# One 512-wide pass over the high weights, and joined PSUM pools, in a two-layer decoder trunk

## The chip, the cores and the metric

The kernel runs on one core of a Trainium2 chip. The metric is device time in microseconds (us) of one execution, as the median of several. A profile of one execution shows every instruction of the core's engines: PE (TensorE, matrix products), PEld (its weight loads), DVE (VectorE), ACT (ScalarE), POOL (GpSimd) and SP (SyncE, which issues the DMAs).

## The reference

Two layers act on 256 tokens of width 1024, all in fp32. Each layer is a half-step gated feed-forward block (FFN), a parallel mixer of three branches, and a second FFN, each followed by a layer norm of the residual sum:

```python
for i in range(DEPTH):                                   # DEPTH = 2
    x = layer_norm(DN_ALPHA * x + 0.5 * swiglu(x, ffn1_gate[i], ffn1_up[i], ffn1_down[i]), ...)
    h = x @ w_in[i]                                      # 1024 -> 6144 columns
    z_gmlp, z_qk, z_v, z_s5, z_gate = jnp.split(h, SPLIT_IDX, axis=-1)
    y_a = gmlp_mixer(z_gmlp, ...)                        # causal spatial gating
    y_b = diff_attention(q, k, v, lam, ...)              # 4 heads, two softmaxes each
    y_c = s5_mixer(z_s5, ...)                            # state space, then y * sigmoid(y @ glu_w + glu_b)
    proj = jnp.einsum('blkw,kwd->blkd', jnp.stack([y_a, y_b, y_c], axis=2), w_branch[i])
    mix = jnp.sum(jax.nn.sigmoid(z_gate) * proj, axis=2) @ w_out[i]
    x = layer_norm(DN_ALPHA * x + mix, ...)
    x = layer_norm(DN_ALPHA * x + 0.5 * swiglu(x, ffn2_gate[i], ffn2_up[i], ffn2_down[i]), ...)
```

`swiglu` is `(silu(x @ wg) * (x @ wu)) @ wd` with an inner width of 2816.

## The kernel before

**Split products.** Every fp32 operand of a large product is split into a high part, rounded to the matrix engine's fp32r form, and a low part, the rest. A product of x and w is then three: low x by high w, high x by high w, high x by low w. The weights come from memory as 202 "pairs" of 1 MB (`fetch`, tile `raw`); ACT rounds each to `wh` (`round_hi`, two instructions of 128x1024), and DVE subtracts to get `wl` (`round_lo`, two of 128x1024). `wh` and `wl` have rings of four pairs, so these run some pairs ahead of PE.

**Three forms of product.** `xstat` and `kdown` keep the activations stationary and move 512 weight columns. `wstat`, the subject of the change, keeps a 128x128 block of weights stationary and moves the 256 tokens. For one block of 128 output features it runs over the K-tiles (8 of them for a depth of 1024, 4 for 512), with three products of 256 columns each. Its callers are `couple` (one pair, two blocks: FFN gates `pgc` and ups `puc`, and in the mixer `psu`, `ps5`, `psq` and the gates `psg`), `branch` (`psp`), `glu` (`psl`) and the third branch (`psc`). Two blocks share one PSUM tile of 128x512, and one ACT or DVE instruction takes both out, with the activation function where there is one.

**PSUM.** The eight banks are three pools: `acc` (4), `mm` (2, the products of `wstat`) and `tr` (2, transposes).

**Order.** There are no hand-written queues. Work is written as generators with priorities, and a `Scheduler` with its own cost estimates picks one operation after another and so fixes each engine's order when the program is built. Each engine then runs its list strictly in that order, and waits where an operand isn't there.

**The mixer.** After the columns of `psu`, `ps5` and `psq`, the main stream runs twelve gates `psg`, the branch products `psp`, the GLU product `psl` and the third branch `psc` in the order of the table `GATES`, then the output product (`ac` from `mix`). Beside it, attention (`pss`, `tra`, `po`, `tro`) and the state-space branch put work on DVE, ACT and PE. The state-space branch has four stages: `bu` on PE; on DVE four products `t` per half, two sums, the scans `gr` and `gi`, then `u`, `v` and the states `Hr`, `Hi`; then `py` on PE, eight ACT copies into `y`, and one DVE operation. After the second and the fourth stage `act_y` applies gelu to half of `y` on ACT and splits it; `glu` (`psl`) reads both halves.

Two lines say how the split products of one K-tile stood in `wstat`, and how a gate was taken out:

```python
b += [self.mmul(out, ws[k][0], x[1][:, k, :], k == 0, False),
      self.mmul(out, ws[k][0], x[0][:, k, :], False, False),
      self.mmul(out, ws[k][1], x[0][:, k, :], False, k == n - 1)]
...
yield A.activation(out=e, in_=ps, func=AF.Tanh, scale=0.5)
```

Of the kernel before, what the change touches and what calls it, by code (L numbers as in the profile page):

```python
# [75 lines left out]

def bundle(ops):
    return Op(ops[0].eng, [c for o in ops for c in o.calls], sum(o.cost for o in ops),
              [a for o in ops for a in o.ins], [a for o in ops for a in o.outs])
# [9 lines left out]
class Engine:  # L89
# [210 lines left out]
class Trunk:  # L300
    def __init__(self, ctx, tc, wst, x, lngb, lnt, glngb, s5p, s5bc, wsp, bsp, out):
# [7 lines left out]
        self.mm = pool("mm", bufs=2, space=PSUM)  # L309
        self.tr = pool("tr", bufs=2, space=PSUM)  # L310
# [6 lines left out]
        ya, yb, pl = ("YAh", "YAl"), ("YBh", "YBl"), [("L2", "L3"), ("P2", "P3")]  # L317
# [11 lines left out]
    def ps(self, pool, name, shape=(128, 512)):  # L329
        bufs = 4 if pool is self.acc else 2  # L330
        return Alloc(pool, pool.name, bufs, lambda: pool.tile(list(shape), F32, tag=pool.name, name=name))

    def free(self, *tiles):
        self.s.free(*tiles)


    def slab(self, i, tag, name, dt, bufs):

        if i in self.spare:
            tags = self.spare[i].pop(0)  # L340
            h = []
# [11 lines left out]
    def fetch(self):  # L353
        for i, w in enumerate(self.w):
            w.raw_tiles, w.raw = yield from self.slab(i if i in (2, 3) else -1, "raw", "raw", F32, 2)
            if len(w.raw_tiles) == 1 and i > 1:
# [68 lines left out]

    def couple(self, name):

        p = yield from self.pair()
        out = yield self.ps(self.mm, name, (128, 2, 256))
        for c in range(2):  # L430
            yield from self.wstat(out[:, c, :], self.blocks(p, c, 0, 8), self.xt)
        self.done(p)
        return out
# [91 lines left out]
    def ln_params(self, layer, i, box):  # L525
        for e, tg in enumerate(("P0", "P1")):
            g = yield self.t([128, 1024], tg, "ln" + "gb"[e])
            yield self.GQ.dma_start(out=g, in_=self.lngb[layer, i, e:e + 1, :].partition_broadcast(128))
            box["gb"].append(g)
        box["ev"].set()  # L530

    def norm(self, t, acc, xr, gb, final, evs=None):
# [38 lines left out]
        if t == 0:  # L571
            hi = yield self.t([128, 8, 256], "xh", "xh", F32R)
            lo = yield self.t([128, 8, 256], "xl", "xl", F32R)
            self.xt = (hi, lo)
        self.to_xt(x, t, gb["col"], gb["tr"][t])

    def affine(self, t, x, gb):
# [10 lines left out]
        if gb["left"] == 0:  # L588
            self.free(gain, bias)
# [38 lines left out]
    def ffn(self, layer, which, final):  # L628
# [49 lines left out]
        def gate(c, pg, box, ev):  # L678
            s = yield self.t([128, 2, 256], "t2k", "silc", bufs=3)
            yield A.activation(out=s, in_=pg, func=AF.Silu)  # L680
            self.free(pg)
            yield ev
            yield V.tensor_tensor(out=s, in0=s, in1=box[0], op=ALU.mult)
            self.free(box[0])
# [5 lines left out]
        for c in range(2, 11):  # L690
            pg = yield from self.couple("pgc")
            yield from new_h()
            box, ev = [], Event()
            self.s.spawn(gate(c, pg, box, ev), P_EVAC)
            pu = yield from self.couple("puc")
            box.append(pu)
            ev.set()
# [10 lines left out]
        self.free(*self.xt)  # L708
# [26 lines left out]
    def prep(self, layer, r):  # L735
# [69 lines left out]
        X, C = [], []  # L805
        for z, tg in zip("ri", ("P2", "P3")):
            x = yield self.t([128, 8, 128], tg, "X" + z)
            X.append(x)
        for z, tg in zip("ab", ("YAh", "YAl")):
            x = yield self.t([128, 8, 2, 64], tg, "C" + z)  # L810
            C.append(x)
# [3 lines left out]
        tm = yield self.t([128, 4, 16, 16], "YBh", "s5t4")  # L815
# [60 lines left out]
        self.free(tm, bc)  # L876

        WB = []
        for tg in ("YBh", "YBl"):
            x = yield self.t([128, 4, 2, 128], tg, "WB")  # L880
            WB.append(x)
# [20 lines left out]
        self.free(*WB, *X, *C)  # L902
# [51 lines left out]
    def gmlp(self, r, vn, uT, bsr, ya, evs, ev):  # L954
# [15 lines left out]
        self.free(vn, uT, bsr, r["wsT"])  # L970
        ev.set()

# [18 lines left out]
    def head(self, r, va, e, hs, st):  # L991
# [44 lines left out]
        if st["run"] == 0:  # L1036
            self.free(va)
# [96 lines left out]
    def s5_out(self, r, u5, U2, out):  # L1134
# [32 lines left out]
        self.free(u5, U2, r["k0"])  # L1167
# [10 lines left out]
    def mixer(self, layer, r):  # L1178
# [13 lines left out]
        ggb = []  # L1192
# [3 lines left out]
        def gparams():  # L1196
            for e, tg in enumerate(("P2", "P3")):
                g = yield self.t([128, 512], tg, "gg")
                yield self.GQ.dma_start(out=g, in_=self.glngb[layer, e:e + 1, :].partition_broadcast(128))
                ggb.append(g)  # L1200
# [8 lines left out]
        for t in range(2):  # L1209
            yield self.x_ev[t]  # L1210
            for b in range(2):
# [10 lines left out]
                else:  # L1222
                    if va is None:
                        va = yield self.t([128, 2, 512], "P1", "va")
                    s.spawn(self.evac(ps, va[:, t, :], None, va_ev[t]), P_EVAC)
        def free_gg():
            for e in evs:
                yield e
            self.free(vg, *ggb)
        s.spawn(free_gg(), P_PREP)  # L1230
        uT = yield self.t([128, 4, 256], "P0", "uT")
        evu = [Event(), Event()]
        for c in range(2):
            ps = yield from self.couple("psu")
            s.spawn(self.evac(ps, uT[:, 2 * c:2 * c + 2, :], AF.Gelu_apprx_tanh, evu[c]), P_EVAC)

        yh = yield self.t([128, 4, 256], "YAh", "yah", F32R)
        yl = yield self.t([128, 4, 256], "YAl", "yal", F32R)
        ya, ya_ev = (yh, yl), Event()

        s.spawn(self.gmlp(r, vn, uT, bsr, ya, evs + evu, ya_ev), P_EVAC)
        u5 = yield self.t([128, 4, 256], "P3", "u5")
# [365 lines left out]
```

## Time and profile before

| | us |
|---|---|
| median of 3 runs | 1230.9 (1230.32 to 1231.95) |
| the profiled execution | 1229.86 |
| its span, first to last instruction | 1228.1 |
| PE busy | 1214.4 (99% of the span) |
| DVE busy | 886.3 (72%) |
| ACT busy | 636.8 (52%) |

The profiled execution is 1.0 us below the median, and 1.8 us of it lie outside the span. "Busy" is the time in which at least one instruction of the engine was running; on DVE and ACT an instruction's record overlaps the next one's by a little, so a group's mean is longer than the step from one to the next. Of the span, the first FFN takes until about 201 us, the first mixer until 426, its second FFN until 617; the second layer repeats this.

### The profile page before, as it was taken

How to read it: one execution, taken by the hardware profiler on the slowest of the kernel's cores; microseconds unless marked ns; L12 is line 12 of the kernel's file. 1: busy time of each engine (PE TensorE's matmuls, PEld its weight loads, DVE VectorE, ACT ScalarE, POOL GpSimd, SP SyncE). 2: the span in 40 equal slices, each digit the busy share in tenths (PEclk: the TensorE clock that was granted, in tenths of full speed). 3: DMA queues.
4: the chain of work that ended last, by engine and by line, in shares of the span. 5: the costliest groups of instructions: out<-in, count | busy, mean ns of one | idle time of the engine just before them, and what ended most of it. 6: DMA issues, size and time to landing. Idle time of an engine off the chain costs nothing.

```text
span 1228.1 us, 21124 instructions
## 1 busy us (share of the span) xinstructions
PE 1214.4 (99%) x8734; PEld 1127.6 (92%) x8734; DVE 886.3 (72%) x1564; ACT 636.8 (52%) x980; POOL 16.2 (1%) x52
## 2 busy tenths in 40 slices
PE   8999999999999999999999999999999999999997
PEld 6999998999999889999889999989999998999996
DVE  6887658879996798775685544696899888744446
ACT  6445546567555664454464434376565447534340
POOL 1100000000000020000000000000000000000000
PEclk9999999999999999999999999999999999999999
DMA  8647655463456475766455555456445574655440
GB/s 311 240 174 262 219 205 226 176 247 137 168 202 239 181 258 180 254 227 211 174 204 204 201 175 204 171 200 238 181 146 207 188 240 170 235 180 199 177 171 35
DMA packets 42864, 246.18 MB, mean 200 GB/s; under 512 B 4880, under 2 KB 5648, under 8 KB 17424
## 3 DMA queue, kind: packets, MB, share of 16 engines
q1 hardware_dynamic: 42768, 244.84, 55.4%
q8 instruction: 68, 1.11, 0.4%
q14 instruction: 28, 0.23, 0.1%
HBM read 233.28 MB, written 11.53 MB: 199 GB/s over the span
## 4 chain that ended last, share of the span: by engine, by line
PE 97%; DVE 2%; DMA 0%; ACT 0%; issue 0%; DVEq 0%; SPq 0%
PE ac L203 23%; PE puc L203 17%; PE pgc L203 17%; PE psg L203 11%; PE psq L203 4%; PE psp L203 4%; PE pg L203 4%; PE pu L203 3%; PE psc L203 2%; PE psu L203 2%; PE ps L203 2%; PE pvg L203 2%; PE pva L203 2%; PE py L203 1%; PE psl L203 1%; PE trx L203 1%
## 5 line engine op out<-in xcount | busy, mean ns | idle before, releaser
L203 DVE TENSOR_TENSOR wl<-raw,wh 128x1024 fp32r<-128x1024 f32 (+2 forms) x416 | 481.4, 1190 | 192.6 <-ACT wh L203 185.1
L203 ACT CAST wh<-raw 128x1024 fp32r<-128x1024 f32 (+2 forms) x416 | 410.3, 1022 | 270.6 <-PE ac L203 88.2
L203 PE MATMUL pgc<-xl,wh 128*128 128x256 f32 x576 | 163.7, 284 | 0.0
L203 PE MATMUL puc<-xl,wh 128*128 128x256 f32 x576 | 163.3, 283 | 0.0
L203 PE MATMUL puc<-xh,wl 128*128 128x256 f32 x576 | 163.0, 283 | 0.0
L203 PE MATMUL puc<-xh,wh 128*128 128x256 f32 x576 | 163.0, 283 | 0.0
L203 PE MATMUL pgc<-xh,wh 128*128 128x256 f32 x576 | 163.0, 283 | 0.0
L203 PE MATMUL pgc<-xh,wl 128*128 128x256 f32 x576 | 163.0, 283 | 0.0
L203 PE MATMUL ac<-wh,hTl 128*128 128x512 f32 (+1 forms) x374 | 141.5, 378 | 0.0
L203 PE MATMUL ac<-wh,hTh 128*128 128x512 f32 (+1 forms) x374 | 141.3, 378 | 0.0
L203 PE MATMUL ac<-wl,hTh 128*128 128x512 f32 (+1 forms) x374 | 140.9, 377 | 0.0
L203 PE MATMUL psg<-xl,wh 128*128 128x256 f32 x384 | 111.8, 291 | 0.0
L203 PEld LDWEIGHTS pgc<-xh,wh 128*128 128x128 f32 x576 | 110.4, 192 | 1.0
L203 PEld LDWEIGHTS pgc<-xl,wh 128*128 128x128 f32 x576 | 110.4, 192 | 1.0
L203 PEld LDWEIGHTS puc<-xl,wh 128*128 128x128 f32 x576 | 110.6, 192 | 0.1
L203 PEld LDWEIGHTS puc<-xh,wh 128*128 128x128 f32 x576 | 110.6, 192 | 0.0
L203 PEld LDWEIGHTS puc<-xh,wl 128*128 128x128 f32 x576 | 110.6, 192 | 0.0
L203 PEld LDWEIGHTS pgc<-xh,wl 128*128 128x128 f32 x576 | 110.4, 192 | 0.0
L203 PE MATMUL psg<-xh,wh 128*128 128x256 f32 x384 | 108.6, 283 | 0.0
L203 PE MATMUL psg<-xh,wl 128*128 128x256 f32 x384 | 108.6, 283 | 0.0
L203 PEld LDWEIGHTS ac<-wl,hTh 128*128 128x128 f32 x374 | 70.3, 188 | 13.1
L203 PEld LDWEIGHTS ac<-wh,hTl 128*128 128x128 f32 x374 | 70.5, 188 | 12.3
(263 smaller groups left out, 2312.6 us busy)
## 6 DMA issues: line engine op xcount, KB each, us to landing
raw<-in_wst_dram SPq DMA_DIRECT2D x198, 1024.0 KB, 4.9
raw<-in_wst_dram SPq DMA_DIRECT2D x16, 256.0 KB, 5.4
tbd<-tabw SPq DMA_DIRECT2D x8, 512.0 KB, 6.8
tab<-tbd SPq DMA_DIRECT2D x8, 512.0 KB, 5.6
lng<-in_lngb_dram SPq DMA_DIRECT2D x6, 512.0 KB, 6.4
lnb<-in_lngb_dram SPq DMA_DIRECT2D x6, 512.0 KB, 7.2
wbd<-WB SPq DMA_DIRECT2D x4, 512.0 KB, 7.3
cf<-cd SPq DMA_DIRECT2D x8, 256.0 KB, 5.5
```

The source lines that it names most:

```text
L203: fn(**kw)
```

## The change

The two parts of x stand side by side in one tile (`Duo`: 128 x K-tiles x 2 x 256, low first), so one product of 512 columns does both parts against the high weights. It runs for all K-tiles first; then the 256-wide products with the low weights go on in the half of the PSUM tile that holds the high part. The block's result is the sum of the tile's two halves. `summed` makes it: ACT copies one half out of PSUM into a tile `cp` (128x256), and DVE adds the other half to it. The activation function then reads the sum from SBUF. So a block has a PSUM tile of its own, and each block brings one ACT copy and one DVE add, 280 of each in all.

The pools `mm` and `tr` become one of four tiles. Tiles of SBUF that held high and low parts apart are joined (`YA`, `YB`, `P01`, `P23`, `xx`), with the same work in them. The scheduler's estimate of a product's time is raised from 0.0025 + n/2400 to 0.0133 + n/2400, which moves instructions; the reserve for DMA descriptors is made smaller to give room.

```diff
+class Duo:
+    def __init__(self, tile):
+        self.tile = tile
+        self.parts = (tile[:, :, 1, :], tile[:, :, 0, :])
+    def both(self, k):
+        return self.tile[:, k, :, :]
...
-                return 0.0025 + n / 2400
+                return 0.0133 + n / 2400
...
-        self.mm = pool("mm", bufs=2, space=PSUM)
-        self.tr = pool("tr", bufs=2, space=PSUM)
+        self.mm = self.tr = pool("mm", bufs=4, space=PSUM)
...
-    def wstat(self, out, ws, x):
+    def wstat2(self, out, ws, x):
         n = len(ws)
-        for k0 in range(0, n, 2):
-            b = []
-            for k in (k0, k0 + 1):
-                b += [self.mmul(out, ws[k][0], x[1][:, k, :], k == 0, False),
-                      self.mmul(out, ws[k][0], x[0][:, k, :], False, False),
-                      self.mmul(out, ws[k][1], x[0][:, k, :], False, k == n - 1)]
-            yield bundle(b)
+        for k0 in range(0, n, 4):
+            yield bundle([self.PE.matmul(out=out, lhsT=ws[k][0], rhs=x.both(k), start=k == 0, stop=k == n - 1,
+                                         skip_group_check=True) for k in range(k0, k0 + 4)])
+        for k0 in range(0, n, 4):
+            yield bundle([self.PE.matmul(out=out[:, 0, :], lhsT=ws[k][1], rhs=x[0][:, k, :], start=False,
+                                         stop=k == n - 1, skip_group_check=True) for k in range(k0, k0 + 4)])
+
+    def couple2(self, name, box):
+        p = yield from self.pair()
+        for c in range(2):
+            out = yield self.ps(self.mm, name, (128, 2, 256))
+            yield from self.wstat2(out, self.blocks(p, c, 0, 8), self.xt)
+            box[c].append(out)
+            box[c][0].set()
+        self.done(p)
+
+    def summed(self, box, dst):
+        yield box[0]
+        ps = box[1]
+        cp = yield self.t([128, 256], "cp", "cp", bufs=2)
+        yield self.A.copy(out=cp, in_=ps[:, 0, :])
+        yield self.V.tensor_tensor(out=dst, in0=ps[:, 1, :], in1=cp, op=ALU.add)
+        self.free(ps, cp)
...
-            yield A.activation(out=s, in_=pg, func=AF.Silu)
+            for e in range(2):
+                yield from self.summed(pg[e], s[:, e, :])
+            yield A.activation(out=s, in_=s, func=AF.Silu)
...
+    def evac2(self, box, dst, func, ev, scale=1.0):
+        for e in range(2):
+            yield from self.summed(box[e], dst[:, e, :])
+        if func is not None:
+            yield self.A.activation(out=dst, in_=dst, func=func, scale=scale)
+        ev.set()
...
         def gate(b, m):
-            ps = yield from self.couple("psg" + str(b))
-            s.spawn(tanh(ps, e, ev), P_EVAC)
+            yield from self.couple_to("psg" + str(b), e, AF.Tanh, ev, 0.5)
```

The new order differs in many places; the ones below lie near the end of the first mixer, and the second has the same order there.

Before, on PE, around the last `py` of the state-space branch (the number behind a name is the buffer's):

```order
L203 MATMUL psg1_4145<-xh_2098,wl_3970 128x256
L203 MATMUL py_4179<-Hr_116,cf_4137 64x129 x2
L203 MATMUL py_4179<-Hi_117,cf_4137 64x129 x2
L203 MATMUL py_4179<-Hr_116,cf_4137 64x129 x2
L203 MATMUL py_4179<-U2_2491,k0_1095 32x128 x4
L203 MATMUL py_4179<-Hi_117,cf_4137 64x129 x2
L203 MATMUL psg1_4145<-xl_2099,wh_3938 128x256
L203 MATMUL psg1_4145<-xh_2098,wh_3938 128x256
```

66 products of the gates `psg` follow that `py` before the first `psl`. Now, on PE, at the same place:

```order
L217 MATMUL psg2_3854<-xx_1928,wh_3601 128x512 x8
L217 MATMUL psg2_3854<-xx_1928,wl_3651 128x256 x8
L217 MATMUL py_3915<-Hr_113,cf_3907 64x129 x2
L217 MATMUL py_3915<-Hi_114,cf_3907 64x129 x2
L217 MATMUL py_3915<-Hr_113,cf_3907 64x129 x2
L217 MATMUL py_3915<-uu_2302,k0_1041 32x128 x4
L217 MATMUL py_3915<-Hi_114,cf_3907 64x129 x2
L217 MATMUL psl_3945<-y5d_3198,wh_3680 128x512 x4
L217 MATMUL psl_3945<-y5d_3198,wl_3697 128x256 x4
```

All gates now stand ahead of the last `py`, and `psl`, which reads `y5d` (the split y), comes directly behind it.

Before, on DVE, from the last stage's scan `gi` to `Hi`:

```order
L203 SCALAR_TENSOR_TENSOR gi_3997<-pk_401,t3_3841 128x128 x4
L203 TENSOR_TENSOR u_4059<-gr_3996,tab_3836 128x512
L203 TENSOR_TENSOR v_4060<-gi_3997,tab_3836 128x512
L203 TENSOR_TENSOR wl_4031<-raw_3940,wh_4006 128x1024 x2
L203 TENSOR_TENSOR Hr_116<-u_4059,v_4060 128x4x128
L203 TENSOR_TENSOR u_4102<-gr_3996,tab_3836 128x512
L203 SCALAR_TENSOR_TENSOR part_4110<-th_3755,psp_4076 128x512
L203 TENSOR_TENSOR v_4103<-gi_3997,tab_3836 128x512
L203 SCALAR_TENSOR_TENSOR y5_2945<-u5_2490,spm_211,y5_2945 128x256
L203 TENSOR_TENSOR wl_4122<-raw_4022,wh_4077 128x1024 x2
L203 SCALAR_TENSOR_TENSOR part_4144<-th_4004,psp_4111 128x512
L203 TENSOR_TENSOR Hi_117<-u_4102,v_4103 128x4x128
```

Now, on DVE, the same stage:

```order
L217 TENSOR_TENSOR th_3827<-psg2_3854,cp_3887 128x256
L217 SCALAR_TENSOR_TENSOR gi_3873<-pk_385,t3_3755 128x128 x4
L217 TENSOR_TENSOR u_3899<-gr_3872,tab_3723 128x512
L217 TENSOR_TENSOR v_3900<-gi_3873,tab_3723 128x512
L217 SCALAR_TENSOR_TENSOR y5_2698<-uu_2302,spm_206,y5_2698 128x256
L217 TENSOR_TENSOR Hr_113<-u_3899,v_3900 128x4x128
L217 TENSOR_TENSOR u_3909<-gr_3872,tab_3723 128x512
L217 TENSOR_TENSOR v_3910<-gi_3873,tab_3723 128x512
L217 TENSOR_TENSOR Hi_114<-u_3909,v_3910 128x4x128
L217 TENSOR_TENSOR wl_3904<-raw_3842,wh_3886 128x1024 x2
L217 SCALAR_TENSOR_TENSOR y5_2698<-uu_2302,spm_206,y5_2698 128x256
L217 TENSOR_TENSOR y5d_3198<-y5_2698,y5d_3198 128x2x256
```

The add of `psg2_3854`, the product that stands right ahead of `py` on PE, now stands ahead of `gi`.

Now, on DVE, while PE runs the eight blocks of `psc` and comes to the output product, which reads the first two quarters of `mix` as `mix_4058`:

```order
L217 TENSOR_TENSOR pr_4129<-psc_4127,cp_4143 128x256
L217 TENSOR_TENSOR wl_4152<-raw_4069,wh_4128 128x1024
L217 TENSOR_TENSOR mix_4058<-part_3271,mix_4058 128x2x256
L217 TENSOR_TENSOR pr_4108<-psc_4114,cp_4158 128x256
L217 TENSOR_TENSOR wl_4152<-raw_4069,wh_4128 128x1024
L217 SCALAR_TENSOR_TENSOR th_3207<-th_3207,pr_4108 128x512
L217 TENSOR_TENSOR pr_4129<-psc_4142,cp_4161 128x256
L217 SCALAR_TENSOR_TENSOR part_3303<-th_3207,part_3303 128x512
L217 SCALAR_TENSOR_TENSOR th_3599<-th_3599,pr_4129 128x512
L217 TENSOR_TENSOR wl_4216<-raw_4136,wh_4189 128x1024 x2
L217 TENSOR_TENSOR mix_4058<-part_3303,mix_4058 128x2x256
```

Before, both quarters of that half of `mix` were split ahead of the third and the fourth weight pair of the output product; now both pairs (`wl_4152`, `wl_4216`) stand ahead of the second quarter.

## Rows read from the trace of the kernel before

**Rows 1.** The page's busy time, share of the span and instruction count by engine.
```profile
PE 1214.4 (99%) x8734; PEld 1127.6 (92%) x8734; DVE 886.3 (72%) x1564; ACT 636.8 (52%) x980; POOL 16.2 (1%) x52
```
**Rows 2.** The page's chain that ended last, shares of the span by engine.
```profile
PE 97%; DVE 2%; DMA 0%; ACT 0%; issue 0%; DVEq 0%; SPq 0%
```
**Rows 3.** The chain of waits in order of time: start us, us, what.
```profile
21.09 8.17 PE pu L203 x36
...
50.23 5.75 PE pgc L203 x48
...
61.74 5.47 PE ac L203 x24
```
**Rows 4.** Busy time by stretch: length, PE, PEld, DVE, ACT, POOL, clock, DMA share.
```profile
34.70:104.20 69.50, 69.50 (x550) 65.49 (x550) 57.19 (x145) 32.49 (x44) 0.00 (x0) 1.00 0.63 224
709.00:783.00 74.00, 74.00 (x553) 71.12 (x553) 35.87 (x35) 30.59 (x36) 0.00 (x0) 1.00 0.52 186
223.70:402.80 179.10, 179.02 (x1549) 173.46 (x1549) 147.03 (x305) 102.26 (x197) 0.00 (x0) 1.00 0.55 200
277.30:371.80 94.50, 94.42 (x825) 90.10 (x823) 88.08 (x218) 53.92 (x116) 0.00 (x0) 1.00 0.47 172
```
**Rows 5.** DVE and ACT groups by shape: count | busy us, mean ns of one.
```profile
L203 DVE TENSOR_TENSOR hTl<-trh,hTh 128x256 fp32r<-128x256 f32 x16 | 6.7, 422 | 7.9 <-ACT hTh L203 7.8
...
L203 ACT COPY at<-tra 128x256 f32<-128x256 f32 x8 | 2.9, 368 | 4.6 <-PE tra L203 4.6
```
**Rows 6.** DVE timeline, back-to-back runs of three shapes: start us, us, what.
```profile
279.25 1.74 DVE L203 TENSOR_TENSOR t<-bu,tab 128x256 f32<-128x256 f32 x5
...
288.42 1.29 DVE L203 TENSOR_TENSOR t<-t,t 128x512 f32<-128x512 f32 x2
...
290.08 2.36 DVE L203 TENSOR_TENSOR wl<-raw,wh 128x1024 fp32r<-128x1024 f32 x2
```
**Rows 7.** DVE timeline, third state-space stage, from the scan gi to Hi.
```profile
335.81 1.36 DVE L203 TENSOR_TENSOR_SCAN gi<-pk,t 128x128 f32<-128x128 f32 x4
...
340.59 0.69 DVE L203 TENSOR_TENSOR Hi<-u,v 128x512 f32<-128x512 f32 x1
```
**Rows 8.** The chain of waits from the last py to psl.
```profile
370.07 1.74 PE py L203 x24
371.81 8.11 PE psg L203 x66
379.92 5.65 PE psl L203 x48
```
**Rows 9.** ACT timeline after the last py.
```profile
371.85 2.21 ACT L203 COPY y<-py 32x128 f32<-32x128 f32 x8 [2.89 <-PE py L203]
...
374.69 0.62 ACT L203 ACTIVATE y<-y 128x512 f32<-128x512 f32 x1
...
376.15 0.62 ACT L203 CAST y5h<-y 128x512 fp32r<-128x512 f32 x1
```
**Rows 10.** DVE timeline after the last py.
```profile
374.10 0.49 DVE L203 SCALAR_TENSOR_TENSOR y<-u,spm,y 128x256 f32<-128x256 f32 x1 [3.04 <-ACT y L203]
...
377.42 0.69 DVE L203 TENSOR_TENSOR y5l<-y,y5h 128x512 fp32r<-128x512 f32 x1
```
**Rows 11.** Busy time by stretch at the end of the program.
```profile
1218.00:1222.00 4.00, 1.05 (x9) 0.84 (x8) 2.60 (x10) 0.00 (x0) 0.00 (x0) 1.00 0.00 0
1222.00:1228.00 6.00, 0.00 (x0) 0.00 (x0) 3.06 (x7) 0.00 (x0) 0.00 (x0) 0.57 0.25 87
```
**Rows 12.** PE timeline, the program's first 512-wide products.
```profile
7.60 0.57 PE L203 MATMUL pg<-wh,xl 128*128 128x512 f32 x1
8.01 0.40 PE L203 MATMUL pg<-wh,xh 128*128 128x512 f32 x1
...
9.66 0.40 PE L203 MATMUL pg<-wh,xh 128*128 128x512 f32 x1
9.89 0.40 PE L203 MATMUL pg<-wl,xh 128*128 128x512 f32 x1
```

More of the change, by code (lines that the diff above doesn't have):

```diff
@@ L329, in ps, with duo @@
     def ps(self, pool, name, shape=(128, 512)):
-        bufs = 4 if pool is self.acc else 2
-        return Alloc(pool, pool.name, bufs, lambda: pool.tile(list(shape), F32, tag=pool.name, name=name))
+        return Alloc(pool, pool.name, 4, lambda: pool.tile(list(shape), F32, tag=pool.name, name=name))
+    def duo(self, tag, name, n):
+        x = yield self.t([128, n, 2, 256], tag, name, F32R)
+        return Duo(x)
     def free(self, *tiles):
-        self.s.free(*tiles)
+        self.s.free(*(t.tile if isinstance(t, Duo) else t for t in tiles))
     def slab(self, i, tag, name, dt, bufs):
@@ L525, in ln_params @@
     def ln_params(self, layer, i, box):
[L526 to L529, printed above, removed]
+        g = yield self.t([128, 2, 1024], "P01", "lngb")
+        for e in range(2):
+            yield self.GQ.dma_start(out=g[:, e, :], in_=self.lngb[layer, i, e:e + 1, :].partition_broadcast(128))
+            box["gb"].append(g[:, e, :])
+        box["tile"] = g
         box["ev"].set()
@@ L690, in ffn @@
         for c in range(2, 11):
-            pg = yield from self.couple("pgc")
             yield from new_h()
[L693 to L697, printed above, removed]
+            pg, pu = ([[Event()] for _ in range(2)] for _ in range(2))
+            self.s.spawn(gate(c, pg, pu), P_EVAC)
+            yield from self.couple2("pgc", pg)
+            yield from self.couple2("puc", pu)
             if acc is None:
@@ L1196, in gparams @@
         def gparams():
[L1197 to L1200, printed above, removed]
+            g = yield self.t([128, 2, 512], "P23", "gg")
+            for e in range(2):
+                yield self.GQ.dma_start(out=g[:, e, :], in_=self.glngb[layer, e:e + 1, :].partition_broadcast(128))
+                ggb.append(g[:, e, :])
+            ggt.append(g)
             self.g_ev.set()
@@ L1287, in act_y @@
         def act_y():
-            for nm, tg in (("y5h", "P0"), ("y5l", "P1")):
-                z = yield self.t([128, 4, 256], tg, nm, F32R)
-                zz.append(z)
+            z = yield from self.duo("P01", "y5d", 4)
+            zz.append(z)
             for c in range(2):
@@ L1318, in branch @@
                 m = 2 * m2 + e
-                ps = yield self.ps(self.mm, "psp", (128, 2, 256))
-                for c in range(2):
-                    yield from self.wstat(ps[:, c, :], self.blocks(w, e, 4 * c, 4), (ya, yb)[b])
+                box = [[Event()] for _ in range(2)]
                 if b == 0:
@@ L1344, in glu @@
             w = yield from self.pair()
-            for nm, tg in (("ych", "P2"), ("ycl", "P3")):
-                x = yield self.t([128, 4, 256], tg, nm, F32R)
-                yc.append(x)
+            x = yield from self.duo("P23", "yc", 4)
+            yc.append(x)
             for e in z_ev:
@@ L1389, in mixer @@
         mx = []
-        for tg in (("YAh", "YBh"), ("YAl", "YBl")):
-            x0 = yield self.t([128, 4, 256], tg[0], "mixh", F32R)
-            x1 = yield self.t([128, 4, 256], tg[1], "mixl", F32R)
-            mx.append((x0, x1))
+        for tg in ("YA", "YB"):
+            x = yield from self.duo(tg, "mix", 4)
+            mx.append(x)
         h = []
@@ L1415, in mixer @@
             for mm in range(2):
-                ps = yield self.ps(self.mm, "psc", (128, 2, 256))
-                for c in range(2):
-                    yield from self.wstat(ps[:, c, :], self.blocks(w, mm, 4 * c, 4), yc)
-                s.spawn(third(2 * m2 + mm, ps), P_EVAC)
+                box = [[Event()] for _ in range(2)]
+                s.spawn(third(2 * m2 + mm, box), P_EVAC)
+                yield from self.blocks_to("psc", [self.blocks(w, mm, 4 * c, 4) for c in range(2)], yc[0], box)
             self.done(w)
```

165 lines of the change are left out of this document (84 added, 81 removed).

## The prediction

> **What bounds the kernel now.** I read the busy times first. PE is busy 99% of the span and DVE 72% [rows 1]. A busy PE need not be a PE at its pace, so the second view is the chain that ended last: 97% of it is PE's own work [rows 2]. The third is that chain in order of time, for the step from one product to the next. A run of 48 products of 256 columns takes 5.75 us, 0.1198 each; 24 of 512 columns take 5.47 us, 0.2279 each, and 36 of another 512-wide run 8.17 us, 0.2269 each [rows 3]. Twice the columns do not cost twice the time: two 256-wide products take 0.2396, one 512-wide 0.227 to 0.228. So some 0.012 us of each product are fixed, and fewer, wider products would shorten a kernel that PE bounds.
>
> The last view is busy time by stretch, to see who comes next. In the FFN of the second layer DVE is busy 35.9 of 74.0 us, and 57.2 of 69.5 where the preparation of the state-space tables lies beside the first FFN. In the mixer from `psu` to the output product it is busy 147.0 of 179.1, and from the first scores to the last `py` 88.1 of 94.5 [rows 4]. There DVE is nearly as full as PE, and it is not full of waits.
>
> **What PE saves.** The K-tiles of the stationary-weight products number 2016: 1152 in the FFNs (4 FFNs, 9 chunks, gate and up, 2 blocks of 8) and 432 in each mixer (12 gates, 4 q/k, 2 u and 2 state-space couples of 16, that is 320; `psp` 64, `psc` 32, `psl` 16). Each now costs 3 x 0.1198 = 0.3594, and will cost 0.2269 + 0.1198 = 0.3467 or, by the slower 512-wide run, 0.3477. That saves 0.0117 to 0.0127 us a K-tile, 23.6 to 25.6 us in all. I take 25, as the slow run holds a turn between two matrices that `wstat2` hasn't; 10.7 of it falls in the mixers.
>
> A rule of the Trainium skill speaks against this sum. "TensorE: Matmul & The Clock Gate", section "Wait — 56ns, not 53.3ns?", puts the fixed part of a matmul at about 2.5 ns. By it the change would save 2016 x 2.5 ns = 5 us instead of 25. The two runs above show about 12 ns, so I go by the rows.
>
> **What the evacuation adds.** 280 blocks bring one ACT copy and one DVE add of 128x256 each. The nearest rows are an ACT copy out of PSUM of that shape, 0.368, and a DVE operation of that shape with one operand in PSUM, 0.422 [rows 5]. Back to back, five DVE operations of this shape take 1.74, a step of 0.33 [rows 6]. So DVE gets 280 x 0.33 = 92 us more, ACT some 280 x 0.37 = 104 at most. Silu, tanh and the multiplications stay, with the same sizes. In the FFNs the adds are covered: a chunk has 4, 1.3 us, in the 17 us in which PE does three pairs, and even beside the preparation 57.2 + 16 x 0.33 = 62.5 stay under 69.5 less some 3. `gate`'s result is used two chunks later, and the last chunk's after three pairs of the down product, 8 us, against about 4 us of chain. I cost the FFNs at nothing; if the cover failed, PE would wait at the weights' low parts there. The joined PSUM pool, the joined tiles and the DMA reserve move no work by themselves: nothing.
>
> In each mixer there are 68 blocks, 22.4 us more of DVE: 147.0 + 22.4 = 169.4, in a stretch that PE would now do in 179.1 - 5.3 = 173.8. DVE would have to run at 97% through a chain of waits on other engines. Where this reaches PE is seen in the order. Three places, per layer:
>
> *The last state-space stage.* The add of the gate product `psg2_3854` stands ahead of `gi` on DVE, so `gi` can't start before PE has finished that product; `Hi` needs `gi`; `py` needs `Hi`; `psl` needs the split y; and on PE nothing stands between `psg2_3854`, `py` and `psl`. So this whole chain is a wait of PE. By rows: copy 0.37, add 0.42; from `gi` to the end of `Hi` the third stage has the very same sequence, 335.81 to 340.59 + 0.69, that is 5.47 [rows 7]; the part of `py` (1.74) after its first 4 of 24 records, 1.45 [rows 8]; eight copies 2.21, gelu 0.62 and cast 0.62 on ACT [rows 9]; the y operation 0.49 and the split 0.69 on DVE [rows 10]. Sum 12.34, with eight hand-offs of some 0.06 (371.81 to 371.85, 374.59 to 374.69 [rows 8 to 10]) 12.8. Two `psl` products need only the first half of y, so PE would in the meantime have done `py` and these, 1.74 + 0.46. **Wait: 10.6 us.** Before, the 66 products behind `py` (8.11 us [rows 8]) hid the end of this chain, and `Hi` did not wait for a product just ahead of `py`. The bounds: 9.5 if records overlap more, 12.5 if DVE comes late to the add.
>
> *From `psc` to the output product.* The first `psc` block ends 1.4 us after T, its start, and with the copies DVE begins on its adds at about T + 2.4. Until the second quarter of `mix` is split its list holds 7 adds (0.33), 9 operations of 128x512 (step 0.60) and 6 halves of weight pairs (step 1.17, as half of 2.36) [rows 6]: 2.3 + 5.4 + 7.0 = 14.7, so T + 17.1. PE has eight blocks of 1.39 and one pair of the output product, 24 products in 5.47 for both halves of the tokens, so 2.73 [rows 3]: T + 13.9. It waits 3.2. The fourth quarter comes 2 adds, 5 operations, a cast of 0.62 and a pair later, 6.6, when PE has done two pairs, 5.5: 1.1 more. **Wait: 4.3**, between 2 (ACT ahead, adds earlier) and 6.
>
> *From the first scores to that last stage.* 36 adds, 11.9 us, come in here, PE does 240 K-tiles 2.9 us faster, and DVE has 94.5 - 88.1 = 6.4 us of idle time to give [rows 4]: 8.4 us short. The weight pairs are made some two pairs ahead, which takes up most of it, but attention's transposes are not. **Wait: 2**, between 0 and 8.
>
> *The clock.* PE will stand idle twice for over 4 us around the last `py`. At the end of the program the granted clock is 1.00 up to 1222 us, and 0.57 in the mean after it, when PE had had nothing for three microseconds [rows 11], that is the lower of the two levels for most of it. At the program's start the first 512-wide products follow 0.41 us apart and later ones 0.23 [rows 12]. So the products after these waits may run at 1.2 GHz instead of 2.4 for a while. No row shows for how long after such a wait: between nothing and all 32 K-tiles of `psl` and `psp` at twice the time, 11 us. I take **2**, nearer to the start, where the slow step is gone within 2 us of these products.
> The Trainium skill, "TensorE: Matmul & The Clock Gate", section "What's actually happening", says that an idle PE is throttled to half its clock, and sustained work lifts this; the end of this trace agrees. Without it this term is 0 and the sum 4 us lower.
>
> **The sum.** 1229.86 (the profiled execution) - 25 + 2 x (10.6 + 4.3 + 2 + 2) = 1242.7. The median of the runs lies 1.0 above the profiled one: 1243.7, I say **1244**, 1.1% slower. The change breaks even at waits of 12.5 us a layer. Less than 0.2%, 2.5 us, can't be told from no change.
>
> **The rivals.**
> *Only the last state-space stage costs.* Against 4.3 + 2 + 2 stands that a wait of 10 us lets ACT and the weight pairs run ahead, and what is late behind it may then be hidden. For it: the `mix` wait rests on my counting of steps, and no row shows the two others. Then 1230.9 - 25 + 21.2 = 1227, faster; below 12.5 us a layer it decides the sign. Chance 0.13, including 0.02 for no wait at all (1206), which the order excludes as far as I can see.
> *About even.* One of the smaller terms falls in full: 1228.4 to 1233.4. Chance 0.09.
> *The wide product isn't cheaper.* If the 512-wide product of two parts takes as long as two of 256 columns (0.2396), nothing is saved, the change doesn't do what it says, and the waits remain: 1230.9 + 38 = 1269. The runs in [rows 3] speak against it, though none has stationary weights and 512 columns of x. Chance 0.04. The Trainium skill's 2.5 ns ("TensorE: Matmul & The Clock Gate", section "Wait — 56ns, not 53.3ns?") lies on this side, and would give 1264.
> *DVE bounds the mixers throughout.* If the 32 us of idle time that DVE has in the mixer now [rows 4] all stay, since they are waits on others, the mixer takes 179.1 + 22.4 = 201.5, and PE waits 27.7 a layer: 1230.9 - 25 + 55 = 1261. Chance 0.08.
> The forecast, 1234 to 1257, has 0.66. So slower 0.78, same 0.09, faster 0.13. Low bound: the one-stall case, 1227. High bound: the waits at their upper ends short of the last rival, 1258.
>
> **What would show it.** Right: `pgc` as 8 products of 0.227 and 8 of 0.120 in 2.78 us, FFN chunks of 16.6 us instead of 17.0; on PE, in each mixer, a wait for DVE at `py` of about 5 us and one at `psl` of about 5; waits at `ac` for `mix`; a granted clock under 1 behind them; DVE busy near 980. Wrong: `py` without a wait on `Hi`; a step of 0.24 in the wide pass; PE waiting in the FFNs for `wl`. The forecast is most open in the three small terms, of which I have only bounds.

## The result: 1265.8 us, 2.8% slower

The changed kernel takes 1265.8 us (4 runs, 1263.2 to 1267.2) against 1230.9; the ratio is 1.0283, 95% interval 1.0271 to 1.0295. The forecast was slower, 1244, with a range up to 1258: the sign held and the size did not. The profiled execution took 1267.2, its span 1265.5.

The page's busy times, against [rows 1], and the shares by engine of the chain that ended last, against [rows 2]:

```profile
PE 1214.4 (96%) x6718; PEld 1032.4 (82%) x6718; DVE 983.2 (78%) x1844; ACT 726.8 (57%) x1248; POOL 13.8 (1%) x52
...
PE 64%; DVE 21%; ACT 6%; DMA 6%; issue 2%; SPq 0%; DVEq 0%; ACTq 0%
```

PE has 2016 products fewer and is busy exactly as long: most of what the wide pass saved came back as slower products (8.9 us in each mixer, worked out below). Only 64% of the chain is PE's now, and DVE holds 21% of it. DVE is busy 97 us longer (983.2 - 886.3; 92 were forecast).

Where the 37 us lie is seen by stages. The table gives the time on PE's timeline from the first product of a stage to that of the next: the first FFN (counted from the start of the span), the first mixer (with its output product), the two FFNs between the mixers, the second mixer, and the last FFN up to its last down products.

| us | first FFN | mixer 1 | two FFNs | mixer 2 | last FFN |
|---|---|---|---|---|---|
| before | 200.8 | 224.9 | 379.8 | 224.9 | 166.4 |
| after | 201.6 | 247.9 | 373.4 | 248.1 | 163.1 |

The mixers lose 23 us each, the later FFNs gain 9.7, the first one nothing.

What PE waits for in the first mixer (view of waits: us in total, times, longest). Before, it had no such wait; the last two lines are all that PE waited for in that whole execution:

```profile
PE py L217 <- DVE Hi L217: 10.9, 3, 8.1
...
PE psl L217 <- DVE y5d L217: 3.7, 1, 3.7
...
PE ac L217 <- DVE mix L217: 2.7, 1, 2.7
...
PE trx L203 <- DMA x<-in_x_dram: 4.1, 2, 3.6
PE pg L203 <- DVE xl L203: 0.3, 1, 0.3
```

The chain of waits in order of time (start us, us, what), over the long wait of the first mixer and, last, over a chunk of the third FFN:

```profile
381.98 2.25 DVE wl L217 x2
384.23 0.34 DVE th L217
384.57 1.28 DVE gi L217 x4
...
389.27 0.70 DVE Hi L217
...
390.05 3.21 PE py L217 x24
393.28 0.27 ACT y L217
...
397.34 0.70 DVE y5d L217
398.04 0.04 issue
398.09 4.24 PE psl L217 x14
...
678.36 5.56 PE pgc L217 x32
683.92 5.59 PE puc L217 x32
689.51 5.47 PE ac L217 x24
```

The chunk takes 16.62 us, as forecast (16.6); by [rows 3] two runs of 48 and one of 24 came to 16.97.

Above it is the predicted chain, link for link: the last gate's add (`th`), the scan `gi`, `Hi`, `py`, eight copies, the split y, `psl`. One link was not in it: the halves of a weight pair, 2.25 us, stand ahead of the add. And `py` takes 3.21 us, not 1.74. The stretches around the waits say why; the seventh number of a row is the granted clock:

```profile
275.00:280.00 5.00, 5.00 (x31) 3.84 (x30) 2.80 (x4) 2.16 (x8) 0.00 (x0) 0.54 0.89 329
280.00:284.00 4.00, 4.00 (x22) 2.93 (x22) 2.04 (x11) 2.35 (x4) 0.00 (x0) 0.72 0.71 268
...
382.00:390.00 8.00, 0.00 (x0) 0.00 (x0) 7.97 (x15) 2.98 (x4) 0.00 (x0) 0.66 0.56 194
390.00:393.20 3.20, 3.15 (x25) 2.06 (x25) 2.23 (x2) 0.00 (x0) 0.00 (x0) 0.50 0.02 5
393.20:398.10 4.90, 1.20 (x5) 0.48 (x3) 1.18 (x2) 3.36 (x10) 0.00 (x0) 0.50 0.96 353
398.10:402.00 3.90, 3.90 (x13) 3.32 (x14) 0.42 (x1) 0.88 (x2) 0.00 (x0) 0.54 0.23 95
402.00:406.00 4.00, 4.00 (x25) 3.47 (x24) 2.31 (x5) 2.77 (x7) 0.00 (x0) 1.00 0.01 2
...
428.00:432.00 4.00, 4.00 (x13) 3.13 (x12) 3.96 (x7) 2.52 (x3) 0.00 (x0) 0.62 0.64 246
```

Behind each of three waits (1.9 us at the first `py`, 8.1 at the last, 2.7 at the output product) PE works for a while at a granted clock down to 0.50, the lower of the two levels (1.2 GHz of 2.4). Busy time times (1 - clock), over the six stretches in which PE works at it, gives 2.3 + 1.1 + 1.6 + 0.6 + 1.8 + 1.5 = 8.9 us a layer. (The 0.6 lies ahead of the wait at `psl`, which ends with DVE's split y: at the full clock it would have been spent waiting.)

(A slip in the part on the change: the products with the low weights go on in the half of the PSUM tile that holds low x, `out[:, 0, :]`. No time hangs on it.)

### The profile page after: what moved, and what is told of

Same layout as the page of the kernel before. It is cut to its first block, busy times and chain, and to the rows that moved or that the text cites. A ratio compares the mean times of both kernels' runs of the same rounds, so it can differ in the third digit from the quotient of the medians.

```text
span 1265.5 us, 17840 instructions
## 1 busy us (share of the span) xinstructions
PE 1214.4 (96%) x6718; PEld 1032.4 (82%) x6718; DVE 983.2 (78%) x1844; ACT 726.8 (57%) x1248; POOL 13.8 (1%) x52
## 4 chain that ended last, share of the span: by engine, by line
PE 64%; DVE 21%; ACT 6%; DMA 6%; issue 2%; SPq 0%; DVEq 0%; ACTq 0%
PE ac L217 19%; PE puc L217 12%; PE pgc L217 12%; DVE wl L217 9%; PE psg L217 5%; DMA raw<-in_wst_dram 5%; PE pg L217 4%; PE pu L217 3%; ACT wh L217 2%; PE pvg L217 2%; DVE t L217 2%; PE pva L217 2%; PE py L217 1%; DVE th L217 1%; ACT y L217 1%
## 5 line engine op out<-in xcount | busy, mean ns | idle before, releaser
L217 PE MATMUL puc<-xx,wh 128*128 128x512 f32 x576 | 144.6, 393 | 0.3 <-ACT WB L217 0.3
L217 PE MATMUL pgc<-xx,wh 128*128 128x512 f32 x576 | 143.7, 391 | 0.0
L217 PEld LDWEIGHTS pgc<-xx,wh 128*128 128x128 f32 x576 | 105.1, 188 | 19.9
L217 PEld LDWEIGHTS puc<-xx,wh 128*128 128x128 f32 x576 | 103.6, 189 | 19.2 <-ACT WB L217 0.6
L217 PE MATMUL psg<-xx,wh 128*128 128x512 f32 x384 | 101.9, 404 | 0.0
L217 PEld LDWEIGHTS puc<-xx,wl 128*128 128x128 f32 x576 | 78.4, 190 | 5.5
L217 PEld LDWEIGHTS pgc<-xx,wl 128*128 128x128 f32 x576 | 78.3, 190 | 5.1
L217 PE MATMUL pgc<-xx,wl 128*128 128x256 f32 x576 | 81.3, 283 | 0.0
L217 PE MATMUL puc<-xx,wl 128*128 128x256 f32 x576 | 80.5, 283 | 0.0
L217 PEld LDWEIGHTS ac<-wh,hTh 128*128 128x128 f32 x374 | 70.5, 189 | 11.9
```

What stands on the lines that cost most here:

```text
L217: fn(**kw)
```

## The experiments

Each time is a median against runs of the kernel before on the same chip (1230.5 to 1230.9). The edits are against the changed kernel unless said otherwise.

### One part at a time

**e1, the wide pass in the FFNs only.** The mixers use the old `wstat` and evacuation, on the new tiles and pools.

```diff
 def couple_to(self, name, dst, func, ev, scale=1.0):
-    box = [[Event()] for _ in range(2)]
-    self.s.spawn(self.evac2(box, dst, func, ev, scale), P_EVAC)
-    yield from self.couple2(name, box)
+    ps = yield from self.couple(name)
+    self.s.spawn(self.evac(ps, dst, func, ev, scale), P_EVAC)
```

> The wide pass stays in the FFNs; the mixers' products, evacuations and activations are as before, with the new kernel's joined pools, joined tiles and cost estimate. Theory A (the mixers pay: there the added copies and adds make the state-space chain late, and the FFNs gain): the changed kernel's FFNs are 9 us shorter in all and its mixers 23 us longer each, so here 1230.9 - 9 = 1222, 1219 to 1225. Theory B (the joined pools and tiles or the new cost estimate make the mixers longer, whatever the form of the product): 1230.9 - 9 + 46 = 1268. Theory C (part of the saving in the FFNs is the wide pass of the mixers' weights ahead of them): 1228 to 1231.

Measured: 1229.5, ratio 0.9988 (0.9977 to 0.9999), too little to call a change. The time falls in C's range, but not by C's mechanism: the FFNs gain as said, and the mixers take 229.2 and 229.3, 4.3 more than before, with the old form of product. That is B's direction, at a fifth of its size; e4 and e5 show where it comes from.

**e2, the wide pass in the mixers only.** `gate` in the FFNs takes one tile of two blocks again.

> The wide pass stays in the mixers alone; the FFNs' gate and up products are three 256-wide ones per K-tile again, without copies and adds. Theory A: the mixers still lose 23 us each, so 1230.9 + 46 = 1277, 1272 to 1281. Theory B or a loss that needs both parts (DVE late out of the FFNs): 1250 or less.

Measured: 1275.9, ratio 1.0363 (1.0343 to 1.0383); mixers 246.2 and 246.8. The loss belongs to the mixers alone (A).

**e3, the old estimate in the changed kernel.**

```diff
-                return 0.0133 + n / 2400
+                return 0.0025 + n / 2400
```

> The changed kernel with the scheduler's old estimate of a product, 0.0025 + n/2400, and so with another order. In that order too nothing stands between the last gate, the last two py and psl on PE. Theory A (the late chain of DVE and ACT work is the cause, and the estimate only moves it): 1260 to 1276. Theory B (the new estimate made a bad order): 1245 or less, with waits at py of less than 3 us.

Measured: 1266.7, ratio 1.0285 (1.0268 to 1.0302). The mixers take 249.6 and 250.0: the loss isn't a matter of the estimate. The first FFN takes 196.5 instead of 201.6, though executions differ here: the seven versions with the wide FFNs and the new estimate take 198.5 to 201.6 for it, the six with the old estimate 196.5 to 199.0.

**e4, the new estimate in the kernel before.** The same line, the other way round.

> The kernel of before with the new estimate alone, 0.0133 + n/2400. The four py then stand earlier among the gates, and 102 products of gates and branches more follow the last one before psl. Theory A: PE stays busy and nothing changes by more than 3 us, 1228 to 1234. Theory B: the estimate costs by itself, 1245 or more.

Measured: 1241.3, ratio 1.0086 (1.0071 to 1.0101). The time lies between my two theories: the estimate alone costs 10 us, 4.3 in each mixer, the rest in the first three FFNs (202.9 and 381.0). `py`, `po`, `pss` and `tra` now stand where their operands aren't ready; the clock stays at 1.00 behind these waits. Waits in the first mixer:

```profile
PE py L203 <- DVE Hi L203: 1.3, 1, 1.3
PE po L203 <- ACT at L203: 0.7, 1, 0.7
PE pss L203 <- DVE ast L203: 0.5, 1, 0.5
PE tra L203 <- DVE sm L203: 0.4, 2, 0.3
```

**e5, the wide pass in the FFNs only, with the old estimate** (e1 and e3 together).

> The wide pass in the FFNs alone, as in the first experiment, and the scheduler's old estimate 0.0025 + n/2400, so that the mixers' order is that of before. Theory D (three effects that add up: the FFNs gain 12, the new estimate costs 10, the wide pass in the mixers the rest): the first FFN as with the old estimate in the changed kernel, 196.5 instead of 200.8, the two in the middle 373.8 instead of 379.8, the last 163.1 instead of 166.4, the mixers 224.9 each: 1230.9 - 13.6 = 1217, 1214 to 1220. If the FFNs' gain hangs on the new estimate: 1226 or more.

Measured: **1218.1**, ratio 0.990 (0.9883 to 0.9917), 1.0% faster than before: the best of all versions, as expected (first FFN 196.8, mixers 224.9, two FFNs 373.4, last 163.3). With 224.9 the mixers take what they took before, so the joined pools and tiles cost them nothing; the 4.3 us of e1 were the estimate's. Its busy times:

```profile
PE 1201.4 (99%) x7582; PEld 1066.7 (88%) x7582; DVE 937.2 (77%) x1708; ACT 689.9 (57%) x1124; POOL 15.5 (1%) x52
```

**e12, e5 with each wide product made as two of 256 columns.** The evacuation with its copies and adds stays.

```diff
-    yield bundle([self.PE.matmul(out=out, lhsT=ws[k][0], rhs=x.both(k), ...
+    yield bundle([self.PE.matmul(out=out[:, e, :], lhsT=ws[k][0], rhs=x.both(k)[:, e, :], ...
+                  for k in range(k0, k0 + 4) for e in range(2)])
```

> The kernel with the wide pass in the FFNs and the old estimate (1218.1), but each 512-wide product is made as two of 256 columns into the two halves of the same tile; order, copies, adds and the K-tiles' order stay. Theory W (a fixed 0.012 us of each product is what the wide pass saves): 1152 products more, 1229 to 1234. Rival (the saving comes from the order of the K-tiles, or from the freed waits of the evacuation): 1217 to 1223.

Measured: 1230.3, ratio 1.000 (0.9991 to 1.0009). Theory W: 12.2 us for 1152 products, 10.6 ns each. The chain shows the old steps of a chunk:

```profile
660.93 5.75 PE pgc L217 x48
666.68 5.76 PE puc L217 x48
672.44 5.47 PE ac L217 x24
```

It shows too that the FFNs' 144 copies and adds cost nothing: the time is that of before.

### Which part of the mixer

The next three are e5 with the wide pass in one third of the mixers' products as well, at the old estimate; `couple_to` and `blocks_to` choose by name.

**e9, the gates.**

> The kernel with the wide pass in the FFNs and the old estimate (1218.1), and in the mixers the wide pass with its copies and adds for the gates alone: 192 K-tiles (2.2 us of PE saved) and 24 adds (8 us more of DVE) a layer. In its order psl stands directly behind the last py, and that behind the last gate. Theory O (the uncovered chain costs, whatever DVE's load): a wait of 8 to 12 us at py and psl a layer, and the low clock behind it, 1234 to 1248. Theory L (DVE's load costs, 22 us in all of the mixer's form): a third of it, 1216 to 1226.

Measured: 1254.5, ratio 1.0197 (1.0179 to 1.0216); mixers 242.1 and 243.7. Beyond the upper end of O's range, and far from L. In the first mixer PE waits 4.5 us at the last `py`, less than expected, 3.3 at `psl`, and 2.7 at attention's `tro`, which O did not name.

**e10, u, state space and q/k.**

> As the one before, but the wide pass in the mixers for u, state space and q/k alone: 128 K-tiles (1.5 us saved) and 16 adds (5 us of DVE) a layer. In its order 66 products of gates still follow the last py ahead of psl, as in the kernel of before. Theory O: no wait at py or psl, 1213 to 1219. Theory L: a fourth of the mixers' loss of 48 us, 1224 to 1232.

Measured: 1220.0, ratio 0.9909 (0.9893 to 0.9926), a little above O's range; its interval overlaps that of e5. Theory O of the mixers: they stay at 224.8 and 225.1, although DVE gets 5 us more in each. The 1.5 us of saving is not seen either: waits of 0.8 us at the first `py` and 0.4 at `tra` take most of it. What the profile shows above e5 lies in the FFNs, one wait of 1.8 at `trh` among it.

**e11, the branch products.**

> As the two before, but the wide pass in the mixers for the branch products psp, psl and psc alone: 112 K-tiles (1.3 us saved) and 28 adds (9 us of DVE) a layer. In its order psl again stands directly behind the last py, but the gates' results go through ACT alone, so that no add of the last gate stands ahead of the scan gi. Theory O: the wait at psl of 4 us, one at py of 3 to 8, and the one at the output product, a layer: 1230 to 1246. Theory L: 1218 to 1228.

Measured: 1251.4, ratio 1.0168 (1.0153 to 1.0183), a little above the range of O. Waits from 360 to 450 us:

```profile
PE ac L217 <- DVE mix L217: 5.1, 2, 2.6
PE psl L217 <- DVE y5d L217: 3.7, 1, 3.7
PE py L217 <- DVE Hi L217: 2.5, 1, 2.5
```

So the pass at the gates, with 24 adds, costs 17 to 19 us a mixer, that at the branches, with 28, 16, and that at the columns, with 16, about what it saves. The costs of the parts exceed the 23 us of the whole, as they would if they lengthened the same chain; no run shows that by itself.

### Order or load

**e6, small adds in the same order.** This leaves out most of the low half's part in the mixers' products.

```diff
+        if self.small:   # in the mixers; the scheduler sees the full operations
+            a.calls = self.A.copy(out=dst, in_=ps[:, 1, :]).calls
+            v.calls = self.V.tensor_tensor(out=dst[:, 0:8], in0=ps[:, 0, 0:8], in1=dst[:, 0:8], op=ALU.add).calls
```

> The changed kernel in its own order, instruction for instruction, but in the mixers ACT copies the half of high x straight to its place and DVE adds only 8 of the 256 columns: it leaves out most of the low half's part of the mixers' products, and takes some 0.25 us off each of 68 adds, 17 us of DVE in each mixer. Theory O (order: the chain from the last gate's add over gi, Hi, py and the split y to psl has nothing beside it on PE, however fast DVE is): PE still waits over 5.5 us at the last py and 4 at psl, 1256 to 1264. Theory L (load: DVE's added 22 us make Hi late): the wait at the last py falls under 2 us, 1236 to 1246.

Measured: 1249.2, ratio 1.0154 (1.0139 to 1.0169), between the two. What Theory O said of the waits holds: 7.7 us at the last `py`, and 3.7 at `psl`, where 4 stood. In stretches of the first mixer PE's busy time is 147.7 of 148, then 0.18 of 7.9, then it works at a clock of 0.62; the last two lines are waits of the whole execution:

```profile
224.00:372.00 148.00, 147.70 (x950) 126.39 (x949) 124.51 (x315) 99.77 (x214) 0.00 (x0) 1.00 0.54 192
372.70:380.60 7.90, 0.18 (x4) 0.04 (x2) 7.87 (x15) 2.88 (x4) 0.00 (x0) 0.66 0.56 196
380.60:396.00 15.40, 11.71 (x59) 8.87 (x60) 4.81 (x9) 6.68 (x19) 0.00 (x0) 0.62 0.37 137
...
PE py L217 <- DMA cf<-cd: 15.3, 2, 7.7
PE psl L217 <- DVE y5d L217: 7.4, 2, 3.7
```

So the last wait is the order's: with DVE relieved of 14.6 us (busy 154.0 instead of 168.6 from `psu` to the output product) it is nearly as long as ever. The profile puts it down to the DMA of `cf`, which lands 0.2 us after `Hi`; `Hi` alone would have made it about 7.5. Of the 8 us that each mixer gains, 6.5 lie ahead of that wait, where the first and the third `py` have lost their waits and the low clock: that part was load. ACT's copies are as long here as in the changed kernel; no run takes them out.

**e7, products of no use in the two waits.**

```diff
+                fill = yield self.ps(self.acc, "fill", (128, 512))
+                z = self.xt[0]
+                one = self.mmul(fill[:, 0:256], z[:, 0, 0:128], z[:, 1, :], True, True).calls
+                op.calls = one * 66 + op.calls + one * 28    # around the last py
```

> The changed kernel with products of no use in the two waits: 66 of 256 columns ahead of the last py and 28 behind it, in a PSUM tile that nobody reads, 7.9 and 3.4 us of PE at full clock, a little less than the waits of 8.3 and 4.1. Nothing else moves. Theory K (the low clock behind these waits costs PE some 5 us a layer: py 3.2 instead of 1.7, psl and the first products after it at half pace): 1254 to 1259. Rival: the low clock costs nothing, since the chain behind py is on ACT and DVE: 1264 to 1268; fillers that run over the waits: 1268 or more.

Measured: 1255.2, ratio 1.0195 (1.0180 to 1.0210). Theory K: doing 11 us more of work a layer makes the kernel 10.6 us faster, 9.2 of it in the mixers. PE's timeline has `py` in 1.7 us (388.63 to 390.36) instead of 3.2, and the clock is 1.00:

```profile
388.50:393.80 5.30, 5.19 (x53) 4.66 (x53) 2.87 (x4) 2.69 (x9) 0.00 (x0) 1.00 0.36 110
393.80:400.00 6.20, 5.35 (x30) 4.35 (x29) 2.20 (x5) 2.83 (x7) 0.00 (x0) 1.00 0.61 247
```

Not all of it comes from the two waits. From the end of the last gate to the first `psp` behind `psl` PE takes 19.9 us here in both layers, where the changed kernel takes 23.0 and 22.8: 6.0 us are gained where the edit stands. Another part is chance. In the second layer the first `py`, far from the edit, waits as long as in the changed kernel's first mixer, but the clock stays at 1.00 (the changed kernel's wait, then the wait and the clock here):

```profile
274.82 0.44 PE L217 MATMUL py<-Hi,cf 128*64 128x129 f32 x4 [1.89 <-DVE Hi L217]
...
891.73 0.44 PE L217 MATMUL py<-Hi,cf 128*64 128x129 f32 x4 [1.93 <-DVE Hi L217]
...
887.00:897.00 10.00, 8.07 (x62) 5.94 (x62) 8.65 (x14) 5.35 (x15) 0.00 (x0) 1.00 0.56 193
```

**e8, the state-space branch first.**

```diff
-        self.s.spawn(self.evac2(box, dst, func, ev, scale), P_EVAC)
+        self.s.spawn(self.evac2(box, dst, func, ev, scale), 45)
```

> The changed kernel, in which the copies and adds of the mixers' column products (u, state space, q/k, gates) have a priority behind the state-space branch instead of ahead of it. The order then has the last py some 200 products (6 blocks of gates and 3 of branch pairs) ahead of psl. Theory O: both waits go, 12.4 us a layer and the low clock behind them: 1231 to 1240. Theory L (DVE is the bound of the mixers): PE waits elsewhere, for PSUM tiles or weights, 1250 to 1266.

Measured: 1281.8, ratio 1.0416 (1.0397 to 1.0434). Theory O fell, and the time is above L's range too. The wait at `psl` went, but that at the last `py` did not: PE waits 7.3 us for `Hr` and 1.2 for `Hi` there, 8.5 instead of 8.1. The `py` now stand too early on PE, and it waits at three of the four in each layer, 14.2 us for `Hr` and `Hi`, with stretches of the low clock behind (0.84 in the mean from 290 to 345 us). Both layers together:

```profile
PE py L217 <- DVE Hr L217: 20.2, 4, 7.3
PE py L217 <- DVE Hi L217: 8.1, 6, 1.5
```

**e13, the last gate behind the last py.**

```diff
+            if f == 3:
+                out["py_ev"].set()       # once the last py is issued
...
         for b, m in GATES:
+            if (b, m) == (2, 3):
+                yield so["py_ev"]
```

> The changed kernel with the last gate (32 products, 5.6 us) held back until the last py is issued, so that on PE it stands between py and psl, and on DVE its adds stand behind gi. Theory O (order): Hi no longer waits for that gate's add and the chain from py to psl is covered: the wait at psl goes, the one at py stays near 8, and 4 us with 2 of the low clock go in each layer, 1250 to 1257. Theory L (DVE's load sets when Hi is there): the wait at py grows to 12 or more and the time stays, 1261 to 1269.

Measured: 1258.4, ratio 1.0229 (1.0212 to 1.0246). The time lies between the two ranges, 1.4 us above O's. The last `py` starts 6.6 us earlier in the mixer than in the changed kernel, and `Hi` comes 4.7 earlier, as O says; the wait at `py` stays near 8 (6.4 for `Hr`, 1.2 for `Hi`), and none is left at `psl`. The gate behind it takes 7.1 us, partly at the low clock, where 5.6 were expected. Waits from 360 to 450 us (0.9 of those for `Hi` belong to the third `py`):

```profile
PE py L217 <- DVE Hr L217: 6.4, 1, 6.4
PE ac L217 <- DVE mix L217: 3.6, 1, 3.6
PE py L217 <- DVE Hi L217: 2.1, 2, 1.2
```

**e15, the same in e11.**

> The kernel with the wide pass in the FFNs and the branch products (1251.4), with the last gate (48 products, 5.75 us) held back behind the last py. Theory O: the wait at psl of 4.1 goes, 1239 to 1246. Theory L: Hi comes when it came, the wait at py grows from 2.7 to 8, 1249 to 1256.

Measured: 1242.9, ratio 1.0094 (1.0079 to 1.0109): Theory O. No wait is left at `psl`; PE waits 2.1 us for `Hr` and 1.5 for `Hi` at the last `py`.

**e16, the last two gates behind the last py.**

> As the first of these, with the last two gates (64 products, 11.2 us) held back behind the last py. Theory O: PE reaches py 11 us earlier, and waits there for the third stage's end and the chain of the fourth, of which two gates' adds are taken out, 10 to 13 us; then 11 us of gates cover the way to psl: 1250 to 1258. Theory L: the wait at py grows to 18 or more, 1264 to 1275.

Measured: 1265.5, ratio 1.0290 (1.0253 to 1.0328). The last `py` starts at 179.8 in the mixer instead of 181.9 with one gate held, though PE gets there 7.8 us earlier, and PE waits 12.2 us for `Hr` and 1.2 more for `Hi`:

```profile
PE py L217 <- DVE Hr L217: 12.2, 1, 12.2
```

The verdict is split: the time lies in L's range, the wait at the upper end of O's (10 to 13). From here on the chain itself, on DVE, sets when `py` starts, not the gates.

## Why the prediction was right in sign and wrong in size

**What PE saves: 25 forecast.** The FFNs' part, 1152 x 0.0124 = 14.3, measured 12.2 (e12 against e5): the step of the wide product was 0.0106 us below two narrow ones, not 0.0124. The Trainium skill's 2.5 ns for the fixed part ("TensorE: Matmul & The Clock Gate", "Wait — 56ns, not 53.3ns?") would have been 2.9 us; e12 decides against it, and the rival "the wide product isn't cheaper" is out with it. For the mixers the same step gives 432 x 0.0106 = 4.6 each, an estimate, where I had 5.3.

**The estimate that "moves instructions".** I gave it no price. In the kernel before it costs 10 us (e4), in the changed one it is hidden in the mixers' worse waits (e3), and it takes some of the first FFN's saving. By the ranges given at e3 that is 2 to 3 us; most of the rest of the 5 us by which the FFNs' gain of 9 us falls short of the forecast is that the profiled execution has the longest first FFN of its kind.

**FFNs at nothing.** Right (e12).

**The last state-space stage: 10.6.** Right in place and chain; measured 8.1 + 3.7 = 11.8. I had left out the weight pair ahead of the add (`wl`, 2.25, of which 1.8 behind the copy), and the overlap took some back. The split was not the one I gave (about 5 at `py` and 5 at `psl`): DVE came late to the add, and the slow `py` stands inside the chain. e6 shows the wait at `py` nearly independent of the adds' length, e13 and e15 that a gate between `py` and `psl` removes the part at `psl`.

**From psc to the output product: 4.3.** Measured 2.7.

**From the first scores to that stage: 2.** Measured 2.8, but at other places: 1.9 at the first `py`, ahead of the first scores, and 0.9 at the third. With small adds both are nearly gone (e6), so they hang on DVE's load; but the new estimate's order has a wait of 1.3 at the first `py` without any add (e4), so the load is not their only source.

So the waits were 17.3 a layer where 16.9 stood. That the sum fits better than its parts (1.2 more, 1.6 less, 0.8 more) is luck.

**The clock: 2, "between nothing and 11".** This is the term that failed: 8.9 a layer. I took the value nearest to the program's start [rows 12] and counted one place. Those rows did not bear it out: the profile gives a granted clock of 1.00 for that stretch, 7 to 10 us, so the slow step there isn't shown to be the clock's. In the changed kernel the low clock follows each of three waits, the shortest of 1.9 us at the first `py` included; there the two rows make (5.00 x 0.46 + 4.00 x 0.28) / 0.5 = 6.8 us at the low level. e7 tests two of the three waits: kept busy in them, PE gains 3.0 us a layer, near the 1.6 + 1.8 that the rows give for them. The 3.4 behind the first `py` and the 1.5 behind the output product rest on the rows alone, and the first is not sure to come: the same wait had none behind it in the second layer of e7, and one of 1.4 had none in e1.

Sum for a mixer: 17.3 + 8.9 - 4.6 = 21.6 of the 23.1. Of the other 1.5 at most 0.3 are idle time, for PE is idle 226.00 - 208.39 = 17.6 us in this stretch:

```profile
224.00:450.00 226.00, 208.39 (x1226) 174.76 (x1225) 192.45 (x405) 136.44 (x283) 0.00 (x0) 0.94 0.52 180
```

The rest lies in PE's busy time, as if the pass saved less than 4.6 there, and stays unassigned. Against the forecast, 19 of the 24 us that are missing in the profiled execution lie in the mixers (14 of them the clock), 5 in the FFNs.

**The range and the even case.** The upper end, 1258, is not what my terms give: their own upper ends, 12.5, 6, 8 and 11, make 37.5 a layer and a time of 1281, and I stopped short of the last rival. The case "about even" has a slip as well: without one of the smaller terms the sum is 1235 to 1240, not 1228 to 1233.

**The rivals.** "DVE bounds the mixers throughout" named 1261, near the result, and its condition nearly held: from `psu` to the output product DVE is idle 197.60 - 168.59 = 29.0 us, where it was idle 32.

```profile
224.35:421.95 197.60, 182.68 (x1117) 154.19 (x1116) 168.59 (x366) 120.79 (x257) 0.00 (x0) 0.94 0.52 181
```

But that idle time is no fixed amount: in the same stretch it is 26 us in e10 and 39 in e9. And the runs do not bear out the mechanism: the columns take 16 adds with no loss (e10), a gate moved by one place gains 7 us (e13), and 14.6 us of DVE taken out of each mixer bring 8 (e6). Nor is the order alone the cause: with two gates moved, DVE's chain holds `py` (e16), and e8's order, which takes the wait at `psl` away, makes others.

Shown is this. The loss lies in the mixers' products (e2, e5), at the gates and the branches (e9, e11). The waits at the first and the third `py` nearly go when the adds are short; the one at the last `py` does not (e6). The wait at `psl` goes when a gate stands behind the last `py` (e13, e15). And PE runs slowly behind the waits around the last `py`, which costs about 3 us a layer (e7). How much of the last wait a better order would save isn't known: no run had all these waits cured.

## What to carry to other kernels

A saving on a full engine is worth having only where the engine that pays for it has room: the same pass gave 12 us in the FFNs, where four adds lay beside 16 us of products, broke about even at the mixers' columns, and lost 46 in the mixers as a whole, where adds stood in a serial chain. Try such a change stage by stage. Price a wait of PE with the slow products that can follow it: here 17 us of waits a layer brought 9 more, though after two waits of the same length one had slow products behind it and the other none. And a changed cost estimate of a scheduler is a change of its own, to be timed alone.

## What was not expected of the hardware

Products that nobody needs made the kernel faster: 94 of them a layer went with a time 10.6 us shorter, of which 6.0 are seen where they stand. A wait of 1.9 us at a `py` was followed by 9 us of PE at mean clocks of 0.54 and 0.72, with PE busy throughout; another wait of 1.9 us at the same `py` was followed by a clock of 1.00 (e7, second layer).
